# Reciprocal root of the mean square: one product with 128 equal columns and a power over 384 tokens on GpSimd, in place of a column sum and transposes

## The chip, the cores and the metric

The kernel runs on one core of a Trainium2 chip. The metric is the device time of one execution in microseconds, median of several runs. The engines are named as the profile names them: PE is TensorE (matmul), PEld its weight loads, DVE VectorE, ACT ScalarE, POOL GpSimd, SP the queue from which most DMAs are issued. Each engine works through its own instructions in the order in which they stand in its program; semaphores order the engines among each other.

## What is computed

One inference step of a two-layer decoder: a gated linear attention (GLA) layer, then a dilated window cross-attention layer, each followed by a SwiGLU feed-forward network, for 1024 prompt tokens and 64 sample tokens. What the change touches is the root mean square norm, which stands ahead of and behind every block:

```python
def rmsnorm(x, g):
    x32 = x.astype(jnp.float32)
    y = x32 * lax.rsqrt(jnp.mean(x32 * x32, axis=-1, keepdims=True) + EPS)
    return (y * g.astype(jnp.float32)).astype(x.dtype)

# in trunk(), for each layer l (mixer: GLA in layer 0, dilated windows in layer 1)
y = mixer(rmsnorm(h, norm_g[l, 0]))
h = h + rmsnorm(y, norm_g[l, 1])
h = h + rmsnorm(swiglu(rmsnorm(h, norm_g[l, 2]), w_gate_up[l], w_down[l]), norm_g[l, 3])
# in gla_mixer(): o = rmsnorm(o, g_onorm), over the 256 values of each of 4 heads
```

## The kernel before

Activations lie transposed: a tile has 128 features on its partitions and tokens along its free dimension. The 1088 tokens are cut into three chunks `c` of 384, 384 and 320 (`CH`); 1024 features are 8 tiles, so a chunk's activations are lists of 8 tiles. A weight matrix is split into a high and a low part of 32 bit (`wh`, `wl`), activations likewise (`u`), and `mm3` (line 164) makes each product of three matmuls, at lines 166, 169 and 170.

A norm needs for every token the sum of squares over all features, that is over 8 tiles and 128 partitions, and its reciprocal root on every partition, since tokens lie along the free dimension. ACT squares tiles, DVE adds up to four of them (`squares`, or `out_square`, or lines 643 to 645 in the GLA), which leaves one or two accumulator tiles. `rstd_col` (line 195) turns an accumulator into a column: with 128 tokens of it as weights and a column of ones as moving operand, PE leaves the sums of those tokens on 128 partitions, three such products for a chunk, each with one moving column (line 201). DVE makes the mean of the three columns (line 204), and POOL takes the power -0.5 of those 3 elements per partition (line 205). `rstd` (line 208) then spreads the result: three transposes of a broadcast column (line 213) leave it as a row of 384 tokens on all 128 partitions, in the PSUM tile `nrm`, of which there is one. DVE multiplies the activations with it (line 258 in `postnorm`, lines 230 and 232 in `prenorm`, line 664 in the GLA).

`rstd` is called 18 times: in `postnorm` and then `prenorm`, for each of three chunks, at the output projections of both layers (`out_norm`) and behind the first feed-forward network (`finish_norm`). There are 12 accumulators in the GLA (4 heads by 3 chunks), where `gla` (line 522) calls `rstd_col` at its end, and `gla_out` (line 653) makes the transposes and the multiplication within the next head and chunk. `finish_out` (line 1506), behind the second network, uses `rstd_col` alone, three times. The first norm of the kernel (`x_norm`) has its own sums.

The order of the instructions on each engine is fixed when the program is built, by a list scheduler that goes through the code's statements with priorities (evacuations of PSUM are marked as urgent). PSUM has 8 banks: 4 of the ring `aux`, 2 `mm`, 1 `mx`, 1 `nrm`. `self.T()` gives one of 7 temporary tiles of 128x384 that the squares, the normed tiles and the GLA's decay factors share.

Of the kernel before, what the change touches and what calls it, by code (L numbers as in the profile page):

```python
# [7 lines left out]
F32 = mybir.dt.float32  # L8
F32R = mybir.dt.float32r
U8 = mybir.dt.uint8  # L10
AF = mybir.ActivationFunctionType
ALU = mybir.AluOpType

P = 128
D = 1024
# [5 lines left out]
EPS = 1e-6  # L21
CH = [(0, 384), (384, 384), (768, 320)]
TT = [[0, 128, 256], [0, 128, 256], [0, 128, 192]]
# [84 lines left out]
class Kern:  # L108
# [96 lines left out]
        nc.gpsimd.tensor_tensor(out=r, in0=ms, in1=self.mhalf[:, :3], op=ALU.pow)  # L205
        return r

    def rstd(self, acc, c, width):

        p = self.ps("nrm")  # L210
        r = self.rstd_col(acc, c, width, p)
        for j, t0 in enumerate(TT[c]):
            self.nc.tensor.transpose(p[:, t0:t0 + P], r[:, j:j + 1].to_broadcast([P, P]), self.ident)
        return p

    def split_u(self, src, c):

# [5 lines left out]

    def prenorm(self, u, hs, acc, c, g, rb=None):
        nc, n = self.nc, CH[c][1]
        rb = rb or self.rstd(acc, c, D)
        for k in range(KD):
            t = self.T()
            if g is None:
                nc.vector.tensor_mul(t[:, :n], hs[k][:, :n], rb[:, :n])  # L230
            else:
                nc.vector.scalar_tensor_tensor(
                    out=t[:, :n], in0=hs[k][:, :n], scalar=self.gain(g, k), in1=rb[:, :n],
                    op0=ALU.mult, op1=ALU.mult)
            u[k][c] = self.split_u(t, c)
# [12 lines left out]
    def postnorm(self, ys, acc, c, g, hs, keep):  # L248

        nc, n = self.nc, CH[c][1]  # L250
        rb = self.rstd(acc, c, D)
        sq = []
        for k in range(KD):
            x = y = ys[k][:, :n]
            if not keep and c < 2 and NEWY:
                ys[k] = self.Y(c)
                y = ys[k][:, :n]
            nc.vector.scalar_tensor_tensor(out=y, in0=x, scalar=self.gain(g, k), in1=rb[:, :n], op0=ALU.mult, op1=ALU.mult)
            add = nc.vector if k in (1, 3, 5, 7) else nc.gpsimd
            add.tensor_add(y, y, hs[k])  # L260
            self.squares(sq, y, n, k)
            if keep:
                nc.sync.dma_start(out=self.hT[c][k], in_=y)
        return sq


    def setup(self):
        nc, tc, ctx = self.nc, self.tc, self.ctx
        self.base = ctx.enter_context(tc.tile_pool(name="base", bufs=1))
        self.psum = ctx.enter_context(tc.tile_pool(name="psum", bufs=1, space=bass.MemoryType.PSUM))  # L270
        b = self.base
        self.ident = b.tile([P, P], F32, name="ident")
        nc.sync.dma_start(out=self.ident, in_=self.i["c_ident"])
        self.mask8 = b.tile([P, NB], F32, name="mask8")
        self.ones = b.tile([P, 1], F32, name="ones")
        nc.vector.memset(self.ones, 1.0)
        self.mhalf = b.tile([P, 4], F32, name="mhalf")
        nc.vector.memset(self.mhalf, -0.5)
        self.zeros = b.tile([P, 1, 1], F32, name="zeros")
        nc.vector.memset(self.zeros, 0.0)  # L280
        self.hT = [[tc.dram_tile([P, n], F32, name=f"hT{c}_{k}") for k in range(KD)] for c, (_, n) in enumerate(CH)]
        self.oT = [[tc.dram_tile([P, n], F32, name=f"oT{c}_{k}") for k in range(KD)] for c, (_, n) in enumerate(CH)]
        self.bT = [[tc.dram_tile([P, n], F32, name=f"bT{h}_{c}") for c, (_, n) in enumerate(CH)] for h in range(4)]
        self.bs = []
        self.rT = [[tc.dram_tile([P, n], F32, name=f"rT{c}_{k}") for k in range(KD)] for c, (_, n) in enumerate(CH)]
        dt = tc.dram_tile
        self.hr = [[dt([P, D], F32, name=f"hr{c}_{j}") for j in range(3)] for c in range(3)]
        self.kvs = [dt([SEQ, 512], F32, name=f"kvs{g}") for g in range(3)]
        self.kvn = [dt([NB * NS, 512], F32, name=f"kvn{g}") for g in range(3)]
        self.ext = [dt([16, 384], F32, name=f"ext{g}") for g in range(6)]  # L290
        self.og = [[dt([2, P, SEQ], F32, name=f"og{g}_{c}") for c in range(4)] for g in range(3)]
        self.sts = [[dt([SEQ, 8], F32, name=f"sts{g}_{c}") for c in range(4)] for g in range(3)]
        self.qs = [[dt([4, 64, 64], F32, name=f"qs{g}_{c}") for c in range(4)] for g in range(3)]
        self.os = [dt([P, NB * P], F32, name=f"os{g}") for g in range(3)]
        self.sml = b.tile([P, 3, 2, NB], F32, name="sml")
        self.gains = b.tile([P, 78], F32, name="gains")
        self.W = Weights(self)
        self.shifts = self.cache_shifts()
        W, i = self.W, self.i

        def col(src, n0, n=P):
            return W.add(src[:, n0:n0 + n].rearrange("(k p) n -> p k n", p=P), (KD, P), cols=None if n == P else n)

        def col4(src, k0, n0, gain=None):
            return W.add(src[k0 * P:(k0 + 4) * P, n0:n0 + 256].rearrange("(k p) n -> p k n", p=P), (4, 256), gain)

        def col2(src, k0, n0, gain=None):
            return W.add(src[k0 * P:(k0 + 2) * P, n0:n0 + 512].rearrange("(k p) n -> p k n", p=P), (2, 512), gain)

        def row(src, k):  # L310
            return W.add(src[k * P:(k + 1) * P, :].rearrange("p (a n) -> p a n", a=1), (1, D))

        w_in = i["w_in_a"][0]
        self.u_a = col(w_in, 3072, 16)
        self.u_q, self.u_k, self.u_v = [0] * 4, [0] * 4, [0] * 4
        for h in range(4):
            self.u_q[h] = col(w_in, h * P)
            self.u_k[h] = col(w_in, 512 + h * P)
            self.u_v[h] = [col4(w_in, k0, 1024 + h * 256) for k0 in (0, 4)]
        self.u_r = [col(w_in, 2048 + m * P) for m in range(8)]  # L320
        self.u_g, self.u_u, self.u_d = [0, 0], [0, 0], [0, 0]
        self.ffn_units(0, col, row)
        gkv = lambda k0: (lambda j: self.gain(8, k0 + j))
        gq = lambda k0: (lambda j: self.gain(4, k0 + j))
        self.u_kv = [[col2(i["w_kv"], k0, g * 512, gkv(k0)) for k0 in (0, 2, 4, 6)] for g in range(3)]
        self.u_cq = {}
        for g in ORDER:
            for c in range(4):
                self.u_cq[c, g] = [col4(i["w_q_b"][0], k0, g * 1024 + c * 256, gq(k0)) for k0 in (0, 4)]
        self.u_op = [[col4(i["w_o_b"][0], k0, n0) for n0 in range(0, D, 256)] for k0 in (0, EARLY, 0)]  # L330
        self.ffn_units(1, col, row)
# [190 lines left out]
    def gla(self, h, c, q, k, b, vs, S, more, side, rate):  # L522

        nc, n = self.nc, CH[c][1]
# [21 lines left out]
        for li, s in enumerate(LEVELS):  # L546
# [3 lines left out]
            f = self.T()  # L550
# [12 lines left out]
            if s == 64:  # L563
                pl = self.ps("aux")
                for j in range(nt):
                    mm(pl[0:64, j * 64:(j + 1) * 64], lhsT=f[:, j * P:j * P + 64], rhs=f[:, j * P + 64:(j + 1) * P],
                       start=True, stop=True)
# [50 lines left out]
        if sample:  # L618
            nc.sync.dma_start(out=self.o[2][0, 0, h], in_=S)
            for bb in range(NB):  # L620
                Sb = self.H()
                nc.scalar.dma_start(out=Sb[:, :256], in_=self.i["state_gla"][0, bb, h])
                for f in range(2):
                    self.mmc(ch[f], po[f][:, s0 + bb * NS:s0 + (bb + 1) * NS], lhsT=Sb[:, f * P:(f + 1) * P],
                       rhs=qt[:, s0 + bb * NS:s0 + (bb + 1) * NS], start=bb == 0, stop=False)
# [12 lines left out]
        og, sq = [], []  # L638
        for f in range(2):
            o = self.OT()  # L640
            nc.scalar.activation(o[:, :n], po[f][:, :n], AF.Copy)
            sq.append(self.T())
            nc.scalar.activation(sq[f][:, :n], o[:, :n], AF.Square)
            og.append(o)
        nc.vector.tensor_add(sq[0][:, :n], sq[0][:, :n], sq[1][:, :n])
        p = self.ps("nrm")
        self.normed = (h, c, og, p, self.rstd_col(sq[0], c, 256, p))
        return S

    def OT(self):  # L650
# [2 lines left out]
    def gla_out(self):  # L653

        if self.normed is None:
            return
        nc = self.nc
        (h, c, og, p, r), self.normed = self.normed, None
        n = CH[c][1]
        for j, t0 in enumerate(TT[c]):  # L660
            nc.tensor.transpose(p[:, t0:t0 + P], r[:, j:j + 1].to_broadcast([P, P]), self.ident)
        for f in range(2):
            o = og[f]
            nc.vector.scalar_tensor_tensor(out=o[:, :n], in0=o[:, :n], scalar=self.gains[:, 76 + f:77 + f],
                                           in1=p[:, :n], op0=ALU.mult, op1=ALU.mult)
            nc.sync.dma_start(out=self.oT[c][2 * h + f], in_=o[:, :n])
# [1047 lines left out]
```

## Time and profile before

| | |
|---|---|
| time before, median of 3 runs | 3345.87 us (3340.89 to 3353.46) |
| profiled execution, its own time | 3352.04 us |
| its span, first to last instruction | 3350.3 us |
| PE busy | 3262.6 us (97%) |
| DVE busy | 1643.8 us (49%) |
| ACT busy | 1220.1 us (36%) |
| POOL busy | 137.3 us (4%) |
| mean granted TensorE clock | 0.979 |

Busy shares are of the span. Matmuls are pipelined and the profile models their ends, so PE's busy time says that it seldom stands still and not how well it is used; the distance from one matmul's start to the next is the better measure. The granted clock is the share of full speed that TensorE was given in a stretch.

### The profile page before, as it was taken

The numbers are of one execution on the slowest core, as the hardware profiler recorded it, in microseconds if no ns is written. First come the engines' busy times: TensorE is split into PE (matmuls) and PEld (weight loads), VectorE is DVE, ScalarE is ACT, GpSimd is POOL, SyncE is SP. The second block draws the span as 40 slices with busy tenths as digits, with TensorE's granted clock in tenths as the row PEclk, the third lists the DMA queues.
The fourth block names the chain that finished last, engine by engine and source line by source line (L and its number), as shares of the span: only waits on it lengthen the run. The fifth ranks groups of instructions, "written<-read, shape, count | busy, mean of one in ns | idle before, by whom it ended". The sixth has DMA issues, their size and how long they took to land.

```text
span 3350.3 us, 51862 instructions
## 1 busy us (share of the span) xinstructions
PE 3262.6 (97%) x20130; PEld 3095.3 (92%) x20130; DVE 1643.8 (49%) x4041; ACT 1220.1 (36%) x3016; POOL 137.3 (4%) x138
## 2 busy tenths in 40 slices
PE   8999999999999999999999999999989999999999
PEld 7899999999999999977888998887788999999998
DVE  5666554533333333462446555766685333333335
ACT  4533334431111111232576665655654211111113
POOL 0000000000000000010000000011111000000000
PEclk9999999999999999999999998988999999999999
DMA  5122234422222222234323443433442322221203
GB/s 179 41 75 73 79 113 156 126 98 70 95 70 82 92 73 70 101 126 135 100 64 95 122 127 85 119 109 92 125 125 91 111 70 88 87 75 63 61 26 110
DMA packets 362410, 318.12 MB, mean 95 GB/s; under 512 B 91208, under 2 KB 346268, under 8 KB 360732
## 3 DMA queue, kind: packets, MB, share of 16 engines
q1 hardware_dynamic: 348472, 302.07, 29.3%
q10 hardware_dynamic: 13596, 12.34, 1.2%
q8 instruction: 158, 2.59, 0.3%
q14 instruction: 88, 0.72, 0.1%
q0 software_dynamic: 96, 0.39, 0.0%
HBM read 251.44 MB, written 107.33 MB: 107 GB/s over the span
## 4 chain that ended last, share of the span: by engine, by line
PE 47%; ACT 3%; DVE 3%; issue 2%; DMA 1%; POOL 1%; SPq 0%; DVEq 0%; ACTq 0%; POOLq 0%
PE mm L166 5%; PE mm L170 5%; PE mm L169 5%; PE aux L166 5%; PE aux L170 5%; PE aux L169 5%; PE mx L1213 2%; PE aux L154 2%; PE mx L170 1%; PE mx L169 1%; PE aux L1428 1%; PE mx L166 1%; PE mx L1204 1%; PE aux L1174 1%; PE nrm L1204 1%
## 5 line engine op out<-in xcount | busy, mean ns | idle before, releaser
L166 PE MATMUL aux<-u,wh 128*128 128x384 f32 (+1 forms) x2112 | 695.8, 330 | 2.5 <-ACT u L220 2.5
L169 PE MATMUL aux<-u,wh 128*128 128x384 f32 (+1 forms) x2112 | 696.1, 330 | 0.0
L170 PE MATMUL aux<-u,wl 128*128 128x384 f32 (+1 forms) x2112 | 695.4, 330 | 0.0
L166 PE MATMUL mm<-u,wh 128*128 128x384 f32 (+1 forms) x1152 | 409.0, 356 | 12.0 <-ACT u L220 10.0
L166 PEld LDWEIGHTS aux<-u,wh 128*128 128x128 f32 x2112 | 397.5, 188 | 3.5 <-ACT u L220 3.5
L169 PEld LDWEIGHTS aux<-u,wh 128*128 128x128 f32 x2112 | 397.6, 188 | 0.3 <-DVE u L221 0.3
L170 PEld LDWEIGHTS aux<-u,wl 128*128 128x128 f32 x2112 | 397.3, 188 | 0.0
L169 PE MATMUL mm<-u,wh 128*128 128x384 f32 (+1 forms) x1152 | 392.5, 341 | 3.3 <-DVE u L221 3.2
L170 PE MATMUL mm<-u,wl 128*128 128x384 f32 (+1 forms) x1152 | 392.6, 341 | 0.0
L926 DVE TENSOR_TENSOR aux<-g,aux 128x384 f32<-128x384 f32 x132 | 71.4, 541 | 610.7 <-PE aux L170 422.6
L91 ACT ACTIVATE wh<-ws 128x1024 fp32r<-128x1024 f32 (+1 forms) x177 | 184.3, 1052 | 445.3 <-PE aux L169 277.5
L92 DVE TENSOR_TENSOR wl<-ws,wh 128x1024 fp32r<-128x1024 f32 (+1 forms) x177 | 215.3, 1225 | 200.2 <-ACT wh L91 199.8
L166 PEld LDWEIGHTS mm<-u,wh 128*128 128x128 f32 x1152 | 223.4, 194 | 23.1 <-ACT u L220 11.5
L169 PEld LDWEIGHTS mm<-u,wh 128*128 128x128 f32 x1152 | 223.0, 194 | 8.7 <-DVE u L221 4.7
L166 PE MATMUL mm<-h,wh 128*128 128x384 f32 (+1 forms) x704 | 230.4, 328 | 0.0
L169 PE MATMUL mm<-h,wh 128*128 128x384 f32 (+1 forms) x704 | 230.3, 327 | 0.0
L170 PE MATMUL mm<-h,wl 128*128 128x384 f32 (+1 forms) x704 | 230.2, 327 | 0.0
L170 PEld LDWEIGHTS mm<-u,wl 128*128 128x128 f32 x1152 | 223.0, 194 | 2.6 <-issue 0.2
L925 ACT ACTIVATE g<-aux 128x384 f32<-128x384 f32 x132 | 61.9, 469 | 432.2 <-PE aux L170 432.2
L945 DVE TENSOR_TENSOR y<-y,mm 128x384 f32<-128x384 f32 (+1 forms) x320 | 168.7, 530 | 101.5 <-PE mm L170 101.3
L927 ACT ACTIVATE h<-aux 128x384 fp32r<-128x384 f32 x132 | 62.0, 469 | 385.9 <-DVE aux L926 385.9
L1179 DVE CUSTOM_DVE_ANT_0 S<-aux,bias 128x128 f32<-128x128 f32 (+1 forms) x384 | 121.6, 349 | 106.6 <-PE aux L1175 44.6
(311 smaller groups left out, 6051.2 us busy)
## 6 DMA issues: line engine op xcount, KB each, us to landing
ws<-in_w_gate_up_dram SPq DMA_DIRECT2D x88, 512.0 KB
out_dram<-in_cache_win_dram SPq DMA_DIRECT2D x64, 510.0 KB
x<-in_cache_win_dram SPq DMA_DIRECT2D x48, 512.0 KB
ws<-in_w_down_dram SPq DMA_DIRECT2D x44, 512.0 KB
ws<-in_w_in_a_dram SPq DMA_DIRECT2D x24, 512.0 KB
ws<-in_w_q_b_dram SPq DMA_DIRECT2D x24, 512.0 KB
hT<-y SPq DMA_DIRECT2D x48, 192.0 KB
og<-row SPq DMA_DIRECT2D x64, 128.0 KB
```

Of the source, the lines that this page charges most:

```text
L91: nc.scalar.activation(v[1][:, :, :w], v[0][:, :, :w], AF.Copy)
L92: nc.vector.tensor_sub(v[2][:, :, :w], v[0][:, :, :w], v[1][:, :, :w].bitcast(F32))
L154: m = self.nc.tensor.matmul(*args, **kw)
L166: m = mm(out, lhsT=w[0], rhs=x[0], start=start, stop=False)
L169: mm(out, lhsT=w[0], rhs=x[1], start=False, stop=False)
L170: mm(out, lhsT=w[1], rhs=x[0], start=False, stop=stop)
L926: nc.vector.tensor_mul(pu[:, :n], t[:, :n], pu[:, :n])
L927: nc.scalar.activation(h[:, :n], pu[:, :n], AF.Copy)
L945: nc.vector.tensor_add(ys[m][c][:, :n], ys[m][c][:, :n], ps[:, :n])
L1179: nc.vector.tensor_tensor_reduce(s[:, :w], pv, bias[hq][:, :w][:, ::-1], -1.0, 1e38, ALU.add, ALU.min, row[:, hq:hq + 1])
L1204: m = nc.tensor.transpose(pp[:, x * P:(x + 1) * P], pr[hq][:, kt * P:(kt + 1) * P], self.ident)
L1213: m = mm(po, lhsT=v[kt].rearrange("p e d -> p (e d)"), rhs=pT[kt][x], start=x == kt == 0, stop=x == 1 and kt == nk - 1)
```

## The change

The mean square is made by one product per accumulator: the weights are 128 equal columns of 1/1024 (one column `self.mean`, broadcast), the accumulator with its 384 tokens is the moving operand, and the sum arrives on all 128 partitions at once. DVE adds the epsilon to those 128x384 values and writes them into a temporary tile, POOL takes the power -0.5 of the whole tile in place, and that tile takes the place of the PSUM tile in the multiplications. The GLA's squares are scaled by 4 (the scale in the activation is its root) so that the same 1/1024 gives the mean over 256. `rstd_col` stays for `finish_out` alone. In the GLA, the product, the epsilon and the power are now all issued at the end of a step, and `gla_out` only multiplies.

```diff
-    def rstd(self, acc, c, width):
-
+    def rstd(self, acc, c):
+
+
+        nc, n = self.nc, CH[c][1]
         p = self.ps("nrm")
-        r = self.rstd_col(acc, c, width, p)
-        for j, t0 in enumerate(TT[c]):
-            self.nc.tensor.transpose(p[:, t0:t0 + P], r[:, j:j + 1].to_broadcast([P, P]), self.ident)
-        return p
+        accs = acc if isinstance(acc, list) else [acc]
+        for x, a in enumerate(accs):
+            nc.tensor.matmul(p[:, :n], lhsT=self.mean.to_broadcast([P, P]), rhs=a[:, :n], start=x == 0, stop=x == len(accs) - 1)
+        r = self.T()
+        nc.vector.tensor_scalar(r[:, :n], p[:, :n], EPS, None, ALU.add)
+        nc.gpsimd.tensor_tensor(out=r[:, :n], in0=r[:, :n], in1=self.mhalf[:, 0:1].to_broadcast([P, n]), op=ALU.pow)
+        return r
...
-        self.ones = b.tile([P, 1], F32, name="ones")
+        ones = b.tile([P, 2], F32, name="ones")
+        self.ones, self.mean = ones[:, 0:1], ones[:, 1:2]
         nc.vector.memset(self.ones, 1.0)
+        nc.vector.memset(self.mean, 1.0 / D)
...
-            nc.scalar.activation(sq[f][:, :n], o[:, :n], AF.Square)
+            nc.scalar.activation(sq[f][:, :n], o[:, :n], AF.Square, scale=(D / 256) ** 0.5)
...
-        p = self.ps("nrm")
-        self.normed = (h, c, og, p, self.rstd_col(sq[0], c, 256, p))
+        self.normed = (h, c, og, self.rstd(sq[0], c))
...
-        for j, t0 in enumerate(TT[c]):
-            nc.tensor.transpose(p[:, t0:t0 + P], r[:, j:j + 1].to_broadcast([P, P]), self.ident)
```

The built program's order changes on every engine. In the rows that follow the line numbers of the changed kernel stand 4 to 7 higher behind the edit (line 664 is 668, line 230 is 235, line 558 is 565), and the number at a name's end tells tiles apart.

On DVE, in the GLA, at the turn from one step to the next (head 1, chunk 0), this stood behind the mean of the three columns; 558 to 562 are the next step's decay factors, and the multiplication, line 664, follows five rows behind the last row shown:

```order
L204 TENSOR_SCALAR s_2415<-nrm_2411 128x3
L558 TENSOR_TENSOR t_2595<-y_2580 128x3x64
L559 TENSOR_TENSOR t_2595<-y_2580 128x3x64
L558 TENSOR_TENSOR t_2606<-y_2580 128x6x32
L559 TENSOR_TENSOR t_2606<-y_2580 128x6x32
L558 TENSOR_TENSOR t_2617<-y_2580 128x12x16
L561 TENSOR_TENSOR t_2595<-t_2595,y_1810 128x3x64
L562 TENSOR_TENSOR t_2595<-t_2595,y_1783 128x3x64
L561 TENSOR_TENSOR t_2606<-t_2606,y_1810 128x6x32
L562 TENSOR_TENSOR t_2606<-t_2606,y_1783 128x6x32
L559 TENSOR_TENSOR t_2617<-y_2580 128x12x16
L558 TENSOR_TENSOR t_2628<-y_2580 128x24x8
```

At the same place of the changed program, line 217 adds the epsilon and line 668 is the multiplication, which reads the tile that POOL's power leaves:

```order
L217 TENSOR_SCALAR t_2396<-nrm_2394 128x384
L565 TENSOR_TENSOR t_2572<-y_2560 128x3x64
L566 TENSOR_TENSOR t_2572<-y_2560 128x3x64
L565 TENSOR_TENSOR t_2583<-y_2560 128x6x32
L668 SCALAR_TENSOR_TENSOR h_2385<-h_2385,gains,t_2396 128x384
L668 SCALAR_TENSOR_TENSOR h_2389<-h_2389,gains,t_2396 128x384
L568 TENSOR_TENSOR t_2572<-t_2572,y_1802 128x3x64
L569 TENSOR_TENSOR t_2572<-t_2572,y_1775 128x3x64
```

The multiplication has moved from the sixteenth place behind the sums to the fourth, ahead of the decay factors' products.

On DVE behind the first feed-forward network, chunk 0, in `prenorm` (line 230 multiplies, 97 and 928 are work on weights and on the network's hidden tiles), there was:

```order
L191 TENSOR_TENSOR t_13055<-t_13055,t_13072 128x384
L204 TENSOR_SCALAR s_13083<-nrm_13076 128x3
L230 TENSOR_TENSOR t_13090<-y_7442,nrm_13076 128x384
L97 SCALAR_TENSOR_TENSOR wl_13685<-ws_13683,gains,wh_13684 128x512 x2
L221 TENSOR_TENSOR u_13093<-t_13090,u_13092 128x384
```

In the changed program the same place reads (235 multiplies, 930 is the evacuation of a PSUM tile of the network):

```order
L217 TENSOR_SCALAR t_12958<-nrm_12955 128x384
L235 TENSOR_TENSOR t_12961<-y_7329,t_12958 128x384
L235 TENSOR_TENSOR t_12967<-y_7338,t_12958 128x384
L235 TENSOR_TENSOR t_12973<-y_7347,t_12958 128x384
L930 TENSOR_TENSOR aux_13332<-g_13383,aux_13332 128x320
```

Here nothing stands between the epsilon and the first multiplication, before and now, and the evacuation of `aux` stands behind three multiplications.

On PE at the same norm, ahead of the change, the sums (line 201), three matmuls of the network, and the transposes (line 213):

```order
L170 MATMUL aux_13533<-u_7229,wl_12700 128x320
L201 MATMUL nrm_13076<-ones,t_13055 128x1 x3
L166 MATMUL aux_13533<-u_7235,wh_12699 128x320
L169 MATMUL aux_13533<-u_7236,wh_12699 128x320
L170 MATMUL aux_13533<-u_7235,wl_12700 128x320
L213 MATMUL nrm_13076<-ident,s_13084 128x128 x3
L166 MATMUL aux_13534<-u_7193,wh_12729 128x320
```

And in the changed program, the product with equal columns (line 215):

```order
L166 MATMUL aux_13332<-u_7092,wh_12393 128x320
L215 MATMUL nrm_12955<-t_12934,ones 128x384
L169 MATMUL aux_13332<-u_7093,wh_12393 128x320
L170 MATMUL aux_13332<-u_7092,wl_12394 128x320
L166 MATMUL aux_13332<-u_7098,wh_12393 128x320
```

PE no longer has an instruction that waits for POOL itself; what it waits for next is what DVE and ACT make behind the power.

## Rows read from the trace of the kernel before

**Rows 1.** The page, part 1: busy us, share of the span, instructions.
```profile
span 3350.3 us, 51862 instructions
...
PE 3262.6 (97%) x20130; PEld 3095.3 (92%) x20130; DVE 1643.8 (49%) x4041; ACT 1220.1 (36%) x3016; POOL 137.3 (4%) x138
```

**Rows 2.** Groups by line: busy us, mean ns, idle before and its releasers.
```profile
L201 PE MATMUL nrm<-ones,t 128*128 128x1 f32 x252 | 32.3, 244 | 1.7 <-DVE y L258 1.0 <-DVE t L191 0.6
L205 POOL TENSOR_TENSOR s<-s,mhalf 128x3 f32<-128x3 f32 x33 | 29.0, 878 | 2236.2 <-DVE s L204 2212.0 <-DMA kvs<-h 24.2
L213 PE MATMUL nrm<-ident,s 128*128 128x128 f32 x54 | 10.1, 297 | 10.9 <-POOL s L205 10.7
L661 PE MATMUL nrm<-ident,s 128*128 128x128 f32 x36 | 6.1, 278 | 1.9 <-POOL s L205 1.9
L496 DVE TENSOR_SCALAR t<-aux,gains 128x384 f32<-128x384 f32 (+1 forms) x12 | 7.1, 595 | 8.8 <-ACT t L495 8.8
```

**Rows 3.** Timeline of one norm behind the first network: start us, us, instruction.
```profile
1381.89 0.34 PE L166 MATMUL aux<-u,wh 128*128 128x384 f32 x1
...
1382.21 0.80 PE L201 MATMUL nrm<-ones,t 128*128 128x1 f32 x6
...
1382.88 0.42 PE L169 MATMUL aux<-u,wh 128*128 128x384 f32 x1
...
1384.90 0.34 PE L166 MATMUL aux<-u,wh 128*128 128x384 f32 x1
...
1385.66 0.42 PE L169 MATMUL aux<-u,wh 128*128 128x384 f32 x1
...
1385.84 0.16 DVE L204 TENSOR_SCALAR s<-nrm 128x3 f32<-128x3 f32 x1 [1.63 <-PE nrm L201]
...
1386.10 0.34 PE L166 MATMUL aux<-u,wh 128*128 128x384 f32 x1
1386.14 0.85 POOL L205 TENSOR_TENSOR s<-s,mhalf 128x3 f32<-128x3 f32 x1 [702.69 <-DVE s L204]
1387.04 0.30 PEld L213 LDWEIGHTS nrm<-ident,s 128*128 128x128 f32 x3 [0.93 <-POOL s L205]
1387.05 0.54 PE L213 MATMUL nrm<-ident,s 128*128 128x128 f32 x3 [0.61 <-POOL s L205]
...
1387.34 0.42 PE L169 MATMUL aux<-u,wh 128*128 128x384 f32 x1
...
1387.61 0.34 PE L170 MATMUL aux<-u,wl 128*128 128x384 f32 x1
...
1387.62 4.29 DVE L258 SCALAR_TENSOR_TENSOR y<-y,gains,nrm 128x384 f32<-128x384 f32 x8 [1.63 <-PE nrm L213]
...
1388.49 0.34 PE L169 MATMUL aux<-u,wh 128*128 128x384 f32 x1
```

**Rows 4.** Line 661, the GLA's transposes: PE idle before it, us and times.
```profile
  POOL s L205: 5.1, 8
```

**Rows 5.** Timeline: three fp32 products with 384 moving columns, two records each.
```profile
1558.65 2.10 PE L383 MATMUL aux<-h,h 33*16 33x384 f32 x6 [1.01 <-DMA h<-in_c_onehot_dram]
```

**Rows 6.** POOL's instructions by line: ns min/median/max, first and last start, forms.
```profile
L205 POOL TENSOR_TENSOR s<-s,mhalf x33: 848/851/1155, 122.5 to 3341.6; 128x3 f32<-128x3 f32 x33
L1489 POOL TENSOR_TENSOR u<-u,u x8: 737/740/1056, 2457.6 to 2466.1; 128x256 f32<-128x256 f32 x8
L260 POOL TENSOR_TENSOR y<-y,h x8: 997/1018/1267, 567.4 to 641.9; 128x384 f32<-128x384 f32 x8
```

**Rows 7.** Windows: us, busy (instructions) by engine, PEclk, DMA share, GB/s.
```profile
2570.00:2582.00 12.00, 9.54 (x55) 8.44 (x53) 8.83 (x20) 5.19 (x13) 4.54 (x5) 0.93 0.00 0
2582.00:2590.00 8.00, 7.39 (x37) 7.39 (x38) 6.07 (x15) 3.42 (x8) 0.00 (x0) 0.68 0.01 2
2590.00:2597.00 7.00, 6.79 (x44) 5.63 (x43) 1.98 (x4) 4.98 (x12) 0.00 (x0) 1.00 0.35 123
```

More of the change, by code (lines that the diff above doesn't have):

```diff
@@ L225, in prenorm @@
         nc, n = self.nc, CH[c][1]
-        rb = rb or self.rstd(acc, c, D)
+        rb = rb or self.rstd(acc, c)
         for k in range(KD):
@@ L250, in postnorm @@
         nc, n = self.nc, CH[c][1]
-        rb = self.rstd(acc, c, D)
+        rb = self.rstd(acc, c)
         sq = []
@@ L657, in gla_out @@
         nc = self.nc
-        (h, c, og, p, r), self.normed = self.normed, None
+        (h, c, og, p), self.normed = self.normed, None
         n = CH[c][1]
-        for j, t0 in enumerate(TT[c]):
-            nc.tensor.transpose(p[:, t0:t0 + P], r[:, j:j + 1].to_broadcast([P, P]), self.ident)
         for f in range(2):
```

## The prediction

> **What bounds the kernel now.** I read the page's busy shares first, then the groups by line, then the timeline of one norm. PE is busy 97% of the span, DVE 49%, POOL 4% [rows 1]: time is won by taking work or waits from PE, and lost where PE has to stand still. The groups show how much the norms hold of it: 252 records of the column sums, 54 and 36 of the transposes, and 33 powers of 0.85 us on POOL [rows 2]. The timeline shows that the norm is not hidden, since PE runs in order: behind the matmul of 1386.10 it stands until the power that began at 1386.14 is done, and makes the transposes at 1387.05 [rows 3]. POOL is named as the releaser for most of PE's idle time there [rows 2, 4].
>
> **What PE loses.** From the timeline [rows 3], always start to start of the neighbours, less one ordinary matmul. That matmul is (1388.49 - 1387.61) / 5 = 0.176 us, five lying between those two rows. The first accumulator: 1382.88 - 1381.89 - 0.18 = 0.81 us; the second: 1385.66 - 1384.90 - 0.18 = 0.58; I take 0.70. There are 42 accumulators (12 in the GLA, 6 single ones and 12 pairs elsewhere): 29.4 us. Spreading, with the wait for POOL: 1387.34 - 1386.10 - 0.18 = 1.06 us, in 18 places: 19.1. In the GLA the scheduler had put other matmuls between, so three weight loads of 0.30 us together [rows 3] and up to 5.1 us of idle time over the 12 [rows 4] remain: about 0.5 each, 6. In all 54.5 us.
>
> **What PE gains.** One fp32 product with 384 moving columns for each accumulator. The nearest row has three such products, on 33 partitions, in 2.10 us [rows 5]: 0.70 each. 42 of them are 29.4 us. So PE comes out 25 us ahead, and without a wait for POOL in its own queue. Bounds: if equal broadcast columns loaded as slowly as 0.14 us more for each product, 19; if the waits removed count fully, 30.
>
> **DVE.** The epsilon goes over 128x384 values from PSUM instead of 128x3: 0.6 us by the row of line 496 against 0.16 [rows 2, 3], 30 times, 13 us. DVE is half idle, so on PE's path it counts only as latency of the chain. The multiplications read SBUF in place of PSUM, with the same count and shape; I cost that at nothing, covered by DVE's idle half, and 18 x 0.6 = 11 us if that cover is gone. The temporary tile that now holds the root is one of seven; a wait for one is at least nothing and at most one DVE instruction, 0.6 us in 30 places, 18 us. I take nothing for it.
>
> **POOL's power, the term that decides.** Before: 3 elements per partition in 0.85 us. Now 384 (320 in the last chunk), 30 times. No row has a power of that width, so I bound it. Additions on POOL take 740 ns for 256 columns and 1018 for 384 [rows 6]: 2.17 ns a column and 0.18 us fixed. If everything that a power costs beyond an addition were a fixed start, 384 columns would take as an addition does: **1.0 us** (1.7 with the excess of 0.66 us as a start). If all of the excess goes with the columns, it is (851 - 184) / 3 = 222 ns each, and 384 take **86 us**. Between ends so far apart I lean to the row with the same operation, since a power is many steps and an addition one, but three columns say little of a long run: two thirds of the way in ratio, 1.0 x 86^(2/3) = **19.5 us**, 50 ns a column, and 16.3 us for 320.
>
> The Trainium skill, GPSIMD Engine Reference, section 3.1, puts a two-input elementwise instruction at about 2.6 cycles per element, which would be an estimate of 0.83 us for 384 columns at 1.2 GHz. The additions' 2.17 ns a column agree; if it held for the power too, the first rival below would come true. The same page, section 7, speaks against that: a chain of dependent fp32 steps costs 4 cycles for each step and element. No row here shows which of the two a long power follows.
>
> **What waits behind it.** DVE runs in order, and the changed order puts the multiplication that needs the power behind none to three instructions in all 30 places; in the GLA it stood up to 44 behind before, and it has moved ahead of the next step's decay factors. So DVE stands still for nearly the whole power, and with it everything queued there: decay factors, evacuations of PSUM, the low halves of `u`. PE goes on until it needs one of these. I followed the waits of the changed program from each power to the first PE instruction that cannot start without it, and counted the moving columns of the matmuls between the norm's own product and that one, at 0.176 us for 384. This cover is, in microseconds, in the program's order: GLA 3.9, 8.1, 3.0, 3.5, 7.4, 3.0, 3.5, 7.4, 3.0, 23.8, 13.7, 13.7; output projection of layer 0 2.8, 13.0, 8.8, 3.7, 4.2, 2.1; behind its network 15.1, 9.5, 7.5, 16.7, 6.1, 7.3; output projection of layer 1 3.4, 12.9, 16.9, 0.7, 4.2, 2.8. Together 231.7 us, on average 7.7.
>
> Each place costs PE the power, plus some 1.5 us (the epsilon's 0.6, the first multiplication's 4.29 / 8 = 0.54 [rows 3], and hand-overs), less its cover. One place is covered (23.8 against 21.0). The other 19 of 384 tokens and 10 of 320 cost 19 x 21.0 + 10 x 17.8 - 207.9 = 399 + 178 - 208 = **369 us**.
>
> **The clock behind each stall.** Between 2570 and 2582 PE was busy 9.54 us of 12, and in the next 8 us the granted clock was 0.68, so that a part of them ran at the lower of the two levels, 1.2 GHz; from 2590 on it was 1.00 [rows 7]. That is 8 x 0.32 = 2.6 us lost behind a pause shorter than most of those to come. 29 places: **75 us** (between nothing, if each falls outside, and twice that).
>
> **Sum.** The profiled execution's 3352.0 us, its span of 3350.3 [rows 1] and 1.7 around it, less 25, plus 369 and 75: 3771. It lay 6 us above the median of the runs, so I predict **3765 us**, 12.5% slower.
>
> **The rivals.** What the power costs at 384 columns decides, so they are cases of it, worked by the same sum.
> - *Short power, faster.* At 1.0 us only two places still lack cover, by 2 us together: 3352 - 25 + 2 - 6 = 3323 us. For it speaks that the 0.66 us of excess may be a start paid once. Against it: a start as long as 3.5 additions of 3 columns would be odd. It ends on the faster side as long as the power is under 2 us (3329). Chance 0.12.
> - *Break-even.* From 2 to 4.3 us the stalls return just what PE gains: 3329 to 3363 us. Chance 0.09.
> - *Forecast.* From 4.3 to 40 us, that is 11 to 104 ns a column: 3363 to 4346 us; from 8 to 40, which holds most of it, 3449 to 4346. Chance 0.46.
> - *Column by column.* Little of the 0.66 us is a start and a long run is no faster per column: at 60 us 3352 - 25 + 1514 + 78 - 6 = 4913, at the full 86 about 5640. For it speaks that it is the only row of a power; against it that a long run can overlap its columns. Chance 0.27.
> - *The stall is covered.* The power is long, but PE's matmuls are ordered so that the delay of DVE is worked off in its idle half, and PE hardly waits: 3352 - 25 - 6 = 3321 us if nothing is lost, 3351 if it is 1 us in each place. For it: DVE at 49%; against it the covers above, most of them under 8 us, and that the networks' and GLA's matmuls each need DVE's last result. Chance 0.06.
>
> **How the numbers follow.** About 0.5%, 17 us, is what a measurement of this kernel can tell from no change, so 3329 and 3363 part the signs. Faster: the short power 0.12 and a third of the covered case, 0.02: 0.14. Same: 0.09 and 0.04: 0.13. Slower: 0.46 and 0.27: 0.73. The range leaves out the best of the short power below 3325 (0.06) and powers above 61 us (0.14): 3325 to 4950. For the forecast's case alone it is 3450 to 4350.
>
> **What would show it.** In the profile after: a POOL group of 30 powers with `mhalf`, 384 and 320 wide, whose mean is the term above; if it is near 1 us, the first rival holds, and if it is near 80, the fourth. On DVE the multiplications (lines 237, 263, 668 and 235) must have POOL as releaser and an idle time of about 30 powers. PE's idle time must be that less some 200 us, with the granted clock below 1 behind each power in the GLA and the norms. The products of line 215 should take 0.7 us, and nothing on PE should wait for POOL directly. The sum is wrong if the power is right and PE's idle time is not near 369 us (then the cover is the faulty step), or if the clock does not fall in stalls of ten microseconds and more.

## The result: slower by half, 5064 us

The changed kernel takes 5064.35 us (median of 4 runs, 5055.33 to 5067.11), the kernel before 3343.38 on the same chip: a ratio of 1.514, 95% interval 1.512 to 1.516. That lies outside the stated range, 1299 us above the forecast. Of the rivals "column by column" came true, whose sum at 60 us a power was 4913 us.

The page of the kernel after, part 1, and from its part 2 two rows over 40 slices of the span (PE's busy tenths and the granted clock), answering to [rows 1]:

```profile
span 5065.3 us, 51326 instructions
...
PE 3326.6 (66%) x19872; PEld 3142.0 (62%) x19872; DVE 1673.1 (33%) x4042; ACT 1218.3 (24%) x3016; POOL 1864.8 (37%) x138
...
PE   8234334355241599999423399999994321999999
...
PEclk9667667677575799999756699999897665999999
```

PE fell from 97% busy to 66%, and the low stretches are the GLA (slices 2 to 10) and the norms. POOL has 1728 us more work. The groups by line with shapes kept apart give nearly all of it to one instruction, where [rows 2] had 33 powers of 0.85 us:

```profile
L218 POOL TENSOR_TENSOR t<-t,mhalf 128x384 f32<-128x384 f32 x20 | 1231.6, 61581 | 1132.2 <-DVE t L217 1131.6 <-ACT u L225 0.6
L218 POOL TENSOR_TENSOR t<-t,mhalf 128x320 f32<-128x320 f32 x10 | 513.2, 51320 | 301.0 <-ACT h L596 138.6 <-issue 71.9 <-DVE t L217 68.8
```

A power of 384 columns takes 61.6 us and one of 320 51.3: 160 ns a column, almost no start. The 30 together take 1744.8 us, and the span has grown by 5065.3 - 3350.3 = 1715 us. So the price is paid nearly in full. DVE's waits show where (waiting instruction, what it waited for; us in total, times, longest), and PE's waits who stood behind DVE:

```profile
DVE h L668 <- POOL t L218: 689.1, 12, 61.7
DVE y L263 <- POOL t L218: 521.1, 9, 61.7
...
DVE t L237 <- POOL t L218: 350.0, 6, 61.8
```

```profile
PE aux L573 <- DVE t L569: 551.3, 11, 60.9
PE aux L166 <- ACT u L225: 273.3, 5, 62.3
PE nrm L215 <- DVE t L191: 184.0, 9, 64.1
```

Line 668 is the GLA's multiplication by the root, 263 and 237 those of `postnorm` and `prenorm`; with line 235 (174.9 us) they wait 1735 us. Nothing on PE names the power as what it waits for: PE's first matmul of a decay level (line 573) names DVE's line 569, which stands in DVE's order behind line 668. The releaser named is the nearest link and not the cause.

### The profile page after: what moved, and what is told of

The parts are those of the page before. It is cut to its first block, busy times and chain, and to the rows that moved or that the text cites. A ratio compares the mean times of both kernels' runs of the same rounds, so it can differ in the third digit from the quotient of the medians.

```text
span 5065.3 us, 51326 instructions
## 1 busy us (share of the span) xinstructions
PE 3326.6 (66%) x19872; PEld 3142.0 (62%) x19872; DVE 1673.1 (33%) x4042; ACT 1218.3 (24%) x3016; POOL 1864.8 (37%) x138
## 5 line engine op out<-in xcount | busy, mean ns | idle before, releaser
L218 POOL TENSOR_TENSOR t<-t,mhalf 128x384 f32<-128x384 f32 (+1 forms) x30 | 1744.8, 58161 | 1433.2 <-DVE t L217 1200.4
L166 PE MATMUL mm<-u,wh 128*128 128x384 f32 (+1 forms) x1152 | 415.3, 362 | 116.6 <-ACT y L473 103.9
L169 PE MATMUL mm<-u,wh 128*128 128x384 f32 (+1 forms) x1152 | 398.9, 347 | 121.6 <-DVE u L226 121.2
L166 PEld LDWEIGHTS mm<-u,wh 128*128 128x128 f32 x1152 | 229.0, 199 | 129.8 <-ACT y L473 104.6
L169 PEld LDWEIGHTS mm<-u,wh 128*128 128x128 f32 x1152 | 228.5, 198 | 128.1 <-DVE u L226 123.3
L668 DVE SCALAR_TENSOR_TENSOR h<-h,gains,t 128x384 f32<-128x384 f32 (+1 forms) x24 | 13.2, 593 | 689.1 <-POOL t L218 689.1
```

The costliest lines, as they stand in the source:

```text
L166: m = mm(out, lhsT=w[0], rhs=x[0], start=start, stop=False)
L169: mm(out, lhsT=w[0], rhs=x[1], start=False, stop=False)
L218: nc.gpsimd.tensor_tensor(out=r[:, :n], in0=r[:, :n], in1=self.mhalf[:, 0:1].to_broadcast([P, n]), op=ALU.pow)
```

## The experiments

### The price of the power by itself

Into the kernel before, ten POOL instructions are put in the first network, where POOL is idle.

```diff
+        for n in (3, 6, 12, 48, 192, 384):
+            nc.gpsimd.tensor_tensor(out=o[:, :n], in0=t[:, :n], in1=self.mhalf[:, 0:1].to_broadcast([P, n]), op=ALU.pow)
+        nc.gpsimd.tensor_tensor(out=o, in0=t, in1=e, op=ALU.pow)
+        nc.gpsimd.tensor_tensor(out=o[0:16, :192], in0=t[0:16, :192], in1=e[0:16, :192], op=ALU.pow)
+        for n in (3, 384):
+            nc.gpsimd.tensor_tensor(out=o[:, :n], in0=t[:, :n], in1=e[:, :n], op=ALU.add)
```

Expected: 

> The kernel before, with a row of powers put on GpSimd in the first feed-forward network, where GpSimd has nothing to do and nothing waits for it: 3, 6, 12, 48, 192 and 384 columns with the exponent read from one column, 384 with an exponent tile, 16 partitions by 192 columns, and additions of 3 and 384. Theory (the power goes column by column, as 51.3 us at 320 and 61.5 at 384 say: 0.16 us a column and 0.3 us fixed): 0.8, 1.3, 2.2, 8.0, 30.9 and 61.5 us; 61.5 with the exponent tile; 30.9 on 16 partitions, since partitions are worked side by side. Rival 1 (it is the broadcast exponent that slows the wide power): the same with one column, but far less than 61.5 with the tile, near the additions' 1 us. Rival 2 (the power in the changed kernel is slowed by DVE or by what else runs there): clearly less than 61.5 at 384 here, where it runs alone. The whole time stays within 0.5% of the kernel before under all three, since nothing waits.

Measured: 3338.43 us (one run) against 3348.27, inside the scatter of the kernel before, so on an idle POOL the ten cost nothing that can be seen. Its groups on POOL, shapes apart (lines 222 to 224 are powers, 226 the additions):

```profile
L222 POOL TENSOR_TENSOR t<-t,mhalf 128x384 f32<-128x384 f32 x1 | 62.2, 62224 | 0.1
L223 POOL TENSOR_TENSOR t<-t,t 128x384 f32<-128x384 f32 x1 | 61.7, 61704 | 0.1
L224 POOL TENSOR_TENSOR t<-t,t 16x192 f32<-16x192 f32 x1 | 31.0, 31002 | 0.1
L222 POOL TENSOR_TENSOR t<-t,mhalf 128x192 f32<-128x192 f32 x1 | 30.9, 30930 | 0.1
...
L222 POOL TENSOR_TENSOR t<-t,mhalf 128x48 f32<-128x48 f32 x1 | 9.0, 9013 | 0.1
...
L222 POOL TENSOR_TENSOR t<-t,mhalf 128x12 f32<-128x12 f32 x1 | 2.3, 2265 | 0.1
L222 POOL TENSOR_TENSOR t<-t,mhalf 128x6 f32<-128x6 f32 x1 | 1.3, 1321 | 0.1
L226 POOL TENSOR_TENSOR t<-t,t 128x384 f32<-128x384 f32 x1 | 1.0, 1016 | 0.1
L222 POOL TENSOR_TENSOR t<-t,mhalf 128x3 f32<-128x3 f32 x1 | 0.9, 851 | 0.5 <-DVE u L233 0.5
```

From 3 to 6 columns 157 ns each are added, from 6 to 12 again 157; so 3 columns are 0.38 us of start and 0.47 of columns. Only the 48 columns miss that line, 9.0 us where it gives 7.9; why is open. A broadcast exponent and an exponent tile cost the same, and 16 partitions as much as 128: partitions are worked side by side, columns one behind the other. Alone on POOL the power takes what it takes in the changed kernel, so neither rival holds.

The Trainium skill, GPSIMD Engine Reference, section 3.1, has 2.6 cycles for each element of a two-input addition, which is an estimate of 0.83 us for 384 columns at 1.2 GHz. The addition of two tiles took 1.02 us here, near it; the power took over 70 times the estimate.

### What the rest of the change is worth

The power becomes an addition over the same tile.

```diff
-        nc.vector.tensor_scalar(r[:, :n], p[:, :n], EPS, None, ALU.add)
-        nc.gpsimd.tensor_tensor(..., op=ALU.pow)
+        nc.vector.tensor_scalar(r[:, :n], p[:, :n], EPS, 1.0, ALU.add, ALU.min)
+        nc.gpsimd.tensor_tensor(..., op=ALU.add)
```

Expected: 

> The change with an addition in place of the power on GpSimd, same tiles and same waits; the mean square is clipped at 1 so that values stay finite, and no root is taken. Theory (the 30 powers are all of the loss, and the product with equal columns by itself wins PE time): the addition takes 1.0 us and the time is 3300 to 3335 us, 20 us or more under the kernel before. Rival (the change costs by its product, its temporary tile or DVE's order even without a long power): 3360 us or more.

Measured: 3351.97 us, ratio 1.000 (0.999 to 1.002). That lies between the two expectations: the 30 powers are all of the loss, but even a root for almost nothing gains nothing. Its page, part 1, and its groups of the product:

```profile
span 3344.0 us, 51326 instructions
...
PE 3246.3 (97%) x19872; PEld 3068.9 (92%) x19872; DVE 1671.5 (50%) x4042; ACT 1219.4 (36%) x3016; POOL 144.8 (4%) x138
```

```profile
L215 PE MATMUL nrm<-t,ones 128*128 128x384 f32 (+1 forms) x72 | 31.3, 519 | 20.6 <-DVE t L191 20.5
L215 PE MATMUL nrm<-h,ones 128*128 128x384 f32 (+1 forms) x12 | 4.8, 485 | 0.0
```

PE's busy time is 3262.6 - 3246.3 = 16.3 us shorter, but its idle time (span less busy) has gone from 87.7 to 97.7. The products wait 20.5 us for DVE's last sum of squares (line 191); before, PE waited 10.7 us at the transposes for POOL. The span is 6 us shorter, within the scatter of the runs. The two idle times are steady (84.6 and 85.9 us in two other runs with the matmuls of before, 99.3 in the other kernel with an addition, further down), but the busy times move with the granted clock: the run of the prices, with the matmuls of before, has 3252.1 at 0.982. So the 16.3 us are good to some ten.

### A shorter power: is the cover there?

The power is taken of the first 32, or of the first 128, columns only.

```diff
-        nc.gpsimd.tensor_tensor(out=r[:, :n], ..., op=ALU.pow)
+        nc.gpsimd.tensor_tensor(out=r[:, :32], in0=r[:, :32], in1=self.mhalf[:, 0:1].to_broadcast([P, 32]), op=ALU.pow)
```

Expected, 32: 

> The change with the power on the first 32 columns only; the others keep the mean square, clipped at 1. Theory of the cover as predicted (PE has 7.7 us of other matmuls on average before it needs DVE): at a power of 5.4 us the time is about 3395 us. Rival (no cover: each microsecond of the power is one of PE's, less 30 us in all, as the changed kernel's 1745 us of powers and 1715 us of loss suggest): 30 x 5.4 - 30 = 132 us over the kernel before, 3475 us. If the power had a cost beyond its columns, it would not take 5.4 us here.

Expected, 128: 

> The change with the power on the first 128 columns; the others keep the mean square, clipped at 1. The power should take 20.7 us. Theory of the cover as predicted: about 3830 us. Rival (no cover): 30 x 20.7 - 30 = 591 us over the kernel before, 3935 us.

Measured: 3489.78 us (ratio 1.043, 1.040 to 1.046) and 3940.5 us (one run). POOL's group of line 218 in the first and in the second:

```profile
L218 POOL TENSOR_TENSOR t<-t,mhalf 128x32 f32<-128x32 f32 x30 | 163.3, 5443 | 1450.1 <-DVE t L217 1213.7 <-ACT h L596 140.2 <-issue 72.7
```

```profile
L218 POOL TENSOR_TENSOR t<-t,mhalf 128x128 f32<-128x128 f32 x30 | 622.8, 20758 | 1437.4 <-DVE t L217 1192.2 <-ACT h L596 139.2 <-issue 83.7
```

With the addition (17.7 + 7.2 = 24.9 us over the 30) and the full power there are four points. From 24.9 to 163.3 us on POOL the time rises by 138 us, from 163.3 to 622.8 by 451, from 622.8 to 1744.8 by 1124: 1.00, 0.98 and 1.00 us for each microsecond. In the time, a power of 5.4 us, shorter than 16 of the 30 covers that the prediction lists, is paid in full, as the rival without cover had said.

But this slope of one is the sum of two unlike parts. The pages of the two kernels, part 1:

```profile
span 3485.0 us, 51336 instructions
...
PE 3290.7 (94%) x19872; PEld 3111.4 (89%) x19872; DVE 1669.2 (48%) x4042; ACT 1219.2 (35%) x3016; POOL 283.2 (8%) x138
```

```profile
span 3938.4 us, 51330 instructions
...
PE 3315.5 (84%) x19872; PEld 3133.1 (80%) x19872; DVE 1670.0 (42%) x4042; ACT 1217.6 (31%) x3016; POOL 742.2 (19%) x138
```

What each has more than the kernel with the addition, in us (idle is span less busy):

| power of | the 30 powers | PE idle | PE busy | span | granted clock |
|---|---|---|---|---|---|
| 32 columns | 138.4 | 96.6 | 44.4 | 141.0 | 0.962 |
| 128 columns | 597.9 | 525.2 | 69.2 | 594.4 | 0.910 |
| all columns | 1719.9 | 1641.0 | 80.3 | 1721.3 | 0.818 |

PE's idle time grows by 42, 73 and 79 us less than the powers: so much is covered. Its busy time, for the same instructions, grows by about as much, because the granted clock falls (0.981 with the addition). So the rival had the time right and not the reason. By the covers of the prediction, 30 powers of 5.4 us with 1.5 us of hand-overs would have left 54 us of idle time; it is 97. These are single executions. The other kernel with an addition was busy for 3260.5 us and not 3246.3, at a clock of 0.975, so the busy column is good to some 15 us.

PE does work during the powers. These are windows of the kernel after, each from the start to the end of one power (the 4th, 10th, 21st, 22nd and 26th place, the 30 powers being numbered in their order in time), with the sum over all 30; the first figure behind the length is PE's busy time:

```profile
396.54:458.28 61.74, 2.75 (x24) 2.56 (x22) 1.27 (x3) 0.97 (x3) 61.74 (x1) 0.56 0.00 0
...
943.71:1005.23 61.52, 23.05 (x133) 22.73 (x131) 0.00 (x0) 2.46 (x5) 61.52 (x1) 0.72 0.00 0
...
2594.15:2655.67 61.52, 6.72 (x29) 5.08 (x27) 0.00 (x0) 0.00 (x0) 61.52 (x1) 0.60 0.04 15
2670.96:2732.49 61.53, 15.89 (x68) 12.43 (x66) 0.00 (x0) 0.00 (x0) 61.53 (x1) 0.67 0.01 2
...
3933.61:3995.14 61.53, 11.95 (x80) 11.33 (x78) 0.00 (x0) 0.44 (x1) 61.53 (x1) 0.61 0.03 9
...
sum 1744.88, PE 203.86 PEld 187.92 DVE 13.26 ACT 22.91 POOL 1744.79; mean PE 6.80 PEld 6.26 DVE 0.44 ACT 0.76 POOL 58.16
```

This is what the prediction counted, 203.9 us against 231.7, within 1.1 us at every place but two (5.4 for 8.8 and 10.2 for 16.9). Most of it is taken back. Against the kernel with the addition the span is 5065.3 - 3344.0 = 1721.3 us longer. PE's idle time inside the powers is 1744.9 - 203.9 = 1541.0. Its idle time elsewhere is 5065.3 - 3326.6 - 1541.0 = 197.7, 100 more than that kernel has in all. Its busy time is 80.3 us longer, for the same instructions at a lower clock. 1541 + 100 + 80 is the 1721.

Where the 100 and the 80 arise is seen from power to power. The 29 stretches between the powers are together as long after, 2430 us, as with the addition, 2431, though 179 us of PE's work have left them for the powers: PE idles 99 us more there (172.7 against 74.0), and the work that is left takes 79 us more. Five of them, from the end of POOL's instruction to the start of the next one, with the addition and after:

| place | PE's work during the power | with the addition | after | granted clock there, addition and after |
|---|---|---|---|---|
| 4 | 2.8 | 27.9 | 30.1 | 1.00, 0.87 |
| 10 | 23.1 | 41.2 | 29.8 | 1.00, 0.77 |
| 21 | 6.7 | 15.2 | 15.3 | 0.89, 0.61 |
| 22 | 15.9 | 33.7 | 26.3 | 1.00, 0.81 |
| 26 | 12.0 | 15.7 | 15.2 | 1.00, 0.66 |

Place 4 is longer, with less of PE's work in it, at the lower clock. Places 10 and 22 are shorter by about half of the work done ahead. Places 21 and 26 have had 7 and 12 us of PE's work done ahead and are shorter by 0.5 us at most: between `postnorm` and `prenorm` of a chunk runs a chain of 15 us. Its timeline in the kernel after, behind the power of place 21 (start, length, engine, line; idle time before it and releaser in brackets):

```profile
2594.15 61.52 POOL L218 TENSOR_TENSOR t<-t,mhalf 128x384 f32<-128x384 f32 x1 [26.35 <-DVE t L217]
2655.70 2.41 DVE L263 SCALAR_TENSOR_TENSOR y<-y,gains,t 128x384 f32<-128x384 f32 x3 [61.72 <-POOL t L218]
2656.40 1.30 POOL L265 TENSOR_TENSOR y<-y,u 128x384 f32<-128x384 f32 x1 [0.73 <-DVE y L263]
...
2663.97 1.65 PE L215 MATMUL nrm<-t,ones 128*128 128x384 f32 x2 [63.09 <-DVE t L191]
...
2670.26 0.56 DVE L217 TENSOR_SCALAR t<-nrm 128x384 f32<-128x384 f32 x1
...
2670.96 61.53 POOL L218 TENSOR_TENSOR t<-t,mhalf 128x384 f32<-128x384 f32 x1 [3.72 <-DVE t L217]
```

Multiplication, addition of the residual, square, sum, product, epsilon: DVE is busy 12.77 of these 15.29 us, PE 6.99. PE's matmuls of before had lain beside this chain; done earlier, they leave it as long as it was. The kernel with the addition has the same chain, with the same times from row to row within 0.2 us:

```profile
1440.21 2.44 DVE L263 SCALAR_TENSOR_TENSOR y<-y,gains,t 128x384 f32<-128x384 f32 x3 [1.03 <-POOL t L218]
...
1448.54 1.65 PE L215 MATMUL nrm<-t,ones 128*128 128x384 f32 x2 [2.47 <-DVE t L191]
...
1455.33 0.83 POOL L218 TENSOR_TENSOR t<-t,mhalf 128x384 f32<-128x384 f32 x1 [3.52 <-DVE t L217]
```

How much of the 179 us each of the two, chain and clock, would have taken back without the other is not shown.

### The GLA: the multiplication behind the levels

If the chain behind the wait is what counts, moving work ahead of it must help, and moving PE's must not be needed. `OUTAT` puts the GLA's multiplication behind the next step's six decay levels.

```diff
-OUTAT = 0
+OUTAT = 6
```

Expected, with the full power: 

> The changed kernel with one number altered (OUTAT 0 to 6): in the GLA the multiplication by the root is written behind the six decay levels of the next step instead of ahead of them, so that about 26 DVE instructions of those levels, and the DMAs that feed them, no longer stand behind the wait for the power. Theory A (the power is paid in full because it stands ahead of a chain DVE - PE - DVE that is itself as long as PE's work, and work that PE does during the power only empties what it would have done beside that chain): the 10 to 12 us of the chain that now run beside the power come off at each of the 12 places, 120 to 145 us, so about 4920 to 4945 us. Theory B (the work of other engines beside the power is given back by the clock or lost in any case): 5030 to 5070 us. Theory C (the prediction's cover: only PE's own matmuls count, and these stay in the order they have): 5050 to 5070.

Expected, with the power of 32 columns: 

> Root taken of the first 32 columns only (power of 5.4 us; the other columns keep the clipped mean square), and in the GLA the multiplication behind the six decay levels. With the multiplication ahead of them this kernel took 3490 us. Theory A: the 10 us of levels are longer than 5.4 us, so the power is hidden wholly at 12 of the 30 places: 12 x 4.6 = 55 us less, 3430 to 3440. Theory B: 3480 to 3490.

Expected, with the addition (control): 

> An addition in place of the power (no root at all), with the multiplication behind the six levels: the control for the two runs with a late multiplication. With it ahead of the levels this kernel took 3352 us. Theory A and B: 3340 to 3360, since an addition of 0.8 us has nothing to hide; were it 3300 or less, the order itself, and not the power, would be what the other two runs gain.

Measured: 5003.64 us (one run), 3434.35 (ratio 1.025, 1.022 to 1.028) and 3348.43 (1.000, 0.998 to 1.002). With the power of 5.4 us 55 us came off, the number of theory A. In the stretch from the first power to the thirteenth, the GLA, this run and then the one with the early multiplication have:

```profile
122.37:570.23 447.86, 430.94 (x2944) 409.12 (x2943) 253.11 (x708) 169.26 (x362) 65.75 (x12) 0.98 0.29 89
```

```profile
122.28:628.34 506.06, 448.18 (x2944) 426.46 (x2943) 253.19 (x708) 169.80 (x362) 65.35 (x12) 0.94 0.25 79
```

58 us less, 17 of them PE's busy time, at a granted clock of 0.98 in place of 0.94. DVE's waits for the power in the GLA, in the same order:

```profile
DVE h L668 <- POOL t L218: 20.3, 6, 5.6
```

```profile
DVE h L668 <- POOL t L218: 64.7, 12, 5.6
```

So the power is hidden at 6 places and not at 12 as theory A had it, 44 us of waits, and the clock adds its part; that the two together meet the 55 is in part luck. The control says that the order itself brings nothing without a power.

With the full power only 61 us came instead of 120 to 145, between theory A and the other two. From the first power to the thirteenth 51 us are gone (1126.2 to 1075.2); the rest lies behind the GLA, where nothing was changed, in single runs. From power to power the first nine places are 3.3 to 7.7 us shorter, about as much as DVE now does during a power: 8.34 us at place 4, where 1.27 stood. The expectation had counted the waits of that chain of levels as gained too; only DVE's own work in it was. Places 10 to 12 are unchanged within 0.4 us.

### A queue behind the multiplication

At place 10 DVE waited 5.0 us for a load of `bT`, also with the late multiplication. SyncE's queue in the kernel after shows why:

```profile
1005.91 0.85 SPq L670 DMA_DIRECT2D oT<-h  x2
1007.19 1.79 SPq L694 DMA_DIRECT2D rT<-y  x4
1009.08 0.40 SPq L526 DMA_DIRECT2D y<-bT  x1
```

The write of the product (line 670) waits for DVE and through it for the power, and the load that the next step needs stands behind it; in the program before, this load was ahead of the write. The two writes go to another queue:

```diff
-            nc.sync.dma_start(out=self.oT[c][2 * h + f], in_=o[:, :n])
+            nc.gpsimd.dma_start(out=self.oT[c][2 * h + f], in_=o[:, :n])
```

Expected, full power: 

> The changed kernel with the late multiplication in the GLA, and with the two writes of its result put into GpSimd's DMA queue in place of SyncE's. In the run with the late multiplication the tenth place kept its 91.3 us from power to power, and DVE's decay levels there waited 5.0 us, behind the power, for a load of bT that stands behind these writes in SyncE's queue. If the queue is what holds them (theory), the levels of that place run beside its power: 91.3 falls to about 78 to 83 us, the wait of 5.0 us goes, and the other places stay within 1 us; whole time 4985 to 5000 us. If the load was late for another reason (rival), 91.3 stays and the time is 5000 to 5010.

Expected, 32 columns: 

> The same move of the two writes in the kernel with the power of 32 columns (5.4 us) and the late multiplication, which took 3434 us, 87 us above before. In its trace 6 of the 12 multiplications of the GLA still waited for the power, 20 us together. If the queue held the levels at some of those, 5 to 15 us come off: 3420 to 3430. If not, 3430 to 3440.

Measured: 4992.74 us (one run) and 3431.9 (ratio 1.026, 1.024 to 1.028). The 5.0 us wait is gone, and from power to power place 10 fell from 91.3 to 85.8 us, 11 from 133.6 to 129.8, 12 from 80.3 to 77.0. So the queue did hold place 10, by less than expected. The other places were not all within 1 us: the first took 85.8 us for 83.0, so 3 us at a single place of a single run say little. Place 11 fell in the other pair too, from 78.9 to 73.7. For the short power it is no measurable change in the whole time, and the waits of line 668 stayed at 21 us.

### Two versions that might beat both

The root on ScalarE, as exp(-0.5 ln(x + eps)):

```diff
-        nc.vector.tensor_scalar(r[:, :n], p[:, :n], EPS, None, ALU.add)
-        nc.gpsimd.tensor_tensor(..., op=ALU.pow)
+        nc.scalar.activation(r[:, :n], p[:, :n], AF.Ln, bias=self.eps)
+        nc.scalar.activation(r[:, :n], r[:, :n], AF.Exp, scale=-0.5)
```

Expected: 

> The sum by 128 equal columns stays, and the root is taken on ScalarE as exp(-0.5 ln(x + eps)), two activations of 384 columns (about 0.5 us each by the rows of line 189) in place of epsilon on DVE and power on GpSimd. If nothing else is paid, it lies 0.3 us above the kernel with an addition at each place: 3350 to 3365 us. If ScalarE loads a function table for the logarithm and again for the exponential at each place (rows of 1.28 us in the trace before), 2.6 to 3.9 us come on top, and by the full microsecond that each microsecond of the power cost, 3430 to 3470 us.

Measured: 3385.21 us, ratio 1.011 (1.008 to 1.014). The tables are loaded 26 and 27 times; ACT's timeline at one norm:

```profile
1394.23 1.28 ACT L217 ACT_TABLE_LOAD   x1 [1.73 <-PE nrm L215]
1395.52 0.58 ACT L217 ACTIVATE t<-nrm,ones 128x384 f32<-128x384 f32 x1
1396.12 1.28 ACT L218 ACT_TABLE_LOAD   x1
1397.42 0.53 ACT L218 ACTIVATE t<-t 128x384 f32<-128x384 f32 x1
```

The root takes 3.7 us here, where the 384-column power took 61.6. It is the way to keep the change's product, but 38 us slower than the kernel before. It lies between the two cases expected: 33 us above the kernel with the addition, though loads and activations are 100 us of ACT. Where the other part is hidden is open.

The kernel before with the late multiplication alone. Expected: 

> The kernel before with the late multiplication alone (OUTAT 0 to 6), as a version that might beat both. Its power of three columns is short and PE waits for it only 5.1 us in the GLA, so by theory there is nothing to hide: 3340 to 3352 us, no change. By the rival that DVE's order matters even without a long power, 3300 to 3335.

Measured: 3346.67 us, ratio 1.000 (0.999 to 1.002). No version tried beats the kernel before.

## Why the prediction was wrong

**The step that failed is the price of the power**, "two thirds of the way in ratio", 19.5 us for 384 columns and 16.3 for 320. They are 61.6 and 51.3 us. The row it stood on was right and was read too mildly: by the price run 0.47 of the 0.85 us were three columns, 157 ns each. The upper bound, 222 ns a column, put the whole excess over an addition's start on the columns, and the power has a start of its own of 0.38 us. The argument "three columns say little of a long run" had no row behind it, and the range, which ended at a power of 61 us, rested on it.

**The cover was counted rightly and was worth less.** PE did 204 of the 232 us. The prediction's own sign, PE's idle time as long as the powers less some 200 us, holds inside the powers (1541 us) and fails over the span: idle time of 100 us came back behind them, and against the kernel with the addition only 79 us stay covered. The step took a stall as over when PE stands, and never asked whether the chain behind the power, on DVE, ACT and POOL, leaves PE's work any room afterwards. For the GLA the runs show that work moved ahead of the wait is gained; for the 18 places of the norms the chain is read from timelines alone.

**PE's 25 us** are not in the time: with an addition the kernel is as fast as before. In one pair of executions busy time is 16 us shorter and idle time 10 us longer, by a new wait. A product takes 36.1 / 42 = 0.86 us, not 0.70, and its wait for the last accumulator was left out.

**The clock term held in size**: 75 us predicted, 80 us of busy time found. But the sums of the short powers were made with little or nothing of it, and at 5.4 us it is 44 us already. **What waits behind the power** held, line by line; the queue of SyncE was missing in it.

With the measured power the prediction's own sum is 3352 - 25 + (1745 + 45 - 232) + 78 - 6 = 4957, 107 us short. That is some 25 us of PE's gain, 28 of cover not done and 100 of idle time behind the powers, less the 45 of hand-overs, which the kernel with the addition shows to lie inside its unchanged time. Most of the miss is the price: 4957 less the 3765 forecast is 1192 of the 1299 us.

The rivals: a short power fell with the first row. The stall is not covered either, though the late multiplication shows that it can be in large part where a power is shorter than the work put ahead of it.

## What to carry to other kernels

Before a transcendental is widened from a column per token tile to a row of tokens, price it at two widths: what counts for this power on GpSimd is the length along the free dimension, and 128 copies of a value over partitions are free there while 128 times as many columns are not. Work that an engine can do during a stall counts as cover only if the chain behind the stall is shorter than the work that remains; else it is idle time put off. Here the granted clock was lower behind the stalls too (0.87 and less in the table, for 1.00), so cover and clock belong in one sum. And ask of each delayed instruction which DMA it releases, and what stands behind that in the queue.

## What was not expected of the hardware

- The power on GpSimd has no gain from length: 157 ns a column at 3 to 12 columns, 160 at 320 to 384 (only 48 columns lay off, 9.0 us), the same with 16 partitions as with 128.
- In power windows in which PE is busy under 4 us, the granted clock's mean is 0.51 to 0.58: for most of the stall PE stands at the lower level, 1.2 GHz. In the kernel after, the same instructions kept PE busy 80 us longer than with the addition, 79 of it in the stretches between the powers.
- A table load on ScalarE takes 1.28 us, and the activation behind it starts 1.29 to 1.30 us after it did.
